# One 512-column matmul over the upper and lower part of the activations for each upper weight

## The chip, the cores and the metric

The kernel runs on 1 core of one Trainium2 chip. The metric is device time of one execution, in microseconds (us). Before the change it is 1568.76 us, the median of 3 runs (1565.63 to 1576.21).

## The reference, cut to what matters

One decoder block over 256 tokens of width 2048 (batch 1, one layer). All large products are of float32 weights with float32 activations:

```
mod = silu(c) @ w_mod + b_mod                  # six vectors of 2048
h   = rms_norm(x) * (1 + sc1) + sh1
q, k, v, u, gate_a, gate_s = split(h @ w_in)   # 1024 each for q, k, v, u; 2048 for each gate
y_attn = block-sparse attention of q, k, v     # 8 heads of 128
y_ssm  = y * sigmoid(y @ w_glu + b_glu)        # y from a diagonal state-space scan over u
x  = x + g1 * ((sigmoid(gate_a) * (y_attn @ w_attn_br) + sigmoid(gate_s) * (y_ssm @ w_ssm_br)) @ w_out)
h2 = rms_norm(x) * (1 + sc2) + sh2
val, gt = split(causal_conv3(h2 @ w_up))       # 5632 channels each
x  = x + g2 * ((silu(gt) * val) @ w_down)
```

## The kernel before

Activations lie transposed, channels on the 128 partitions and the 256 tokens along the row. To keep float32 accuracy, a product is made of three fp32r matmuls: weights and activations are both split into an upper part (rounded to fp32r) and a lower part (the rest), and upper by upper, upper weight by lower activation and lower weight by upper activation are added up in PSUM.

`chan_block` does this for 512 output channels. It goes over the contraction in steps of 256 rows, each step one weight tile of 128x1024 (512 KB). For each of four groups of 128 output channels (`m`) and two slices of 128 contraction rows (`k`) it issues

```
PE.matmul(p[m], hi[:, k, ms], act_hi(kk), ...)   # L264
PE.matmul(p[m], hi[:, k, ms], act_lo(kk), ...)   # L266
PE.matmul(p[m], lo[:, k, ms], act_hi(kk), ...)   # L268
```

so 24 matmuls of 256 columns in a step, each behind a weight load of its own. `tok_block` (q, k, v) has the activations as weights and the split weight as moving operand, in matmuls of 512 columns (L294 to L299).

The order of work is written out. `plan` holds all weight tiles; `go` takes them in turn. A tile is loaded on SP's queue into one of 5 `raw` buffers (`mraw`, 4 buffers, for the tiles of `w_mod` once the second pool is open), ScalarE makes `whi` (L182, `split_hi`), VectorE makes `wlo` (L187, `split_lo`), three steps ahead of the step that uses them (`WB` = 3). The tiles of `w_mod` are put between the steps at rates (`R_GLU` 0.6, `R_PPP` 0.4, `R_OUT` 0.9, `R_FFN` 0.34 tiles a step). From the GLU on, a tile of `w_mod` is a VectorE multiplication with `cb`, the broadcast silu(c) (L441); `cb` comes by a DMA on POOL's queue (L453). What belongs behind a block (`post`: sigmoid, convolution, gating, splitting the result again) is issued one step after the block's last step. Two PSUM buffers `mm` of 4 KB per partition hold the running block and the one before it. The compiler's scheduler may put instructions of one engine in another order than they are written, by its own time model, and then fixes it.

In order of time: modulation, u, k, q, v and gate_s (until 413 us), gate_a (`gap`), the attention branch (`pap`), the GLU (`glup`), the state-space branch (`ppp`), `w_out` (`outp`), the second norm, then the FFN (`gp` gate, `vp` value, `dp` down) in two halves, from 812 us to the end.

The pool `ssm` (scan) is closed before the GLU and the pool `post` is opened in its space; `cb`, `mraw` and the FFN tiles are in `post`. The 16 `head` tiles (attention) lie in the pool `act`, which stays open.

Of the kernel before, what the change touches and what calls it, by code (L numbers as in the profile page):

```python
# [23 lines left out]
HID = 5632  # L24
# [18 lines left out]
def block_kernel(ctx: ExitStack, tc: tile.TileContext, I, out):  # L43
# [6 lines left out]
    sm = ctx.enter_context(tc.tile_pool(name="sm", bufs=2))  # L50
    ps = ctx.enter_context(tc.tile_pool(name="ps", bufs=1, space=PSUM))
# [16 lines left out]
    def pair(kind, c, name, dt=F32R):  # L68

        return act.tile([128, 2, 256], dt, name=name, tag=f"{kind}{c}", bufs=1)  # L70

    def pairs(kind, c0, n, name):
        tiles = [pair(kind, c, name) for c in range(c0, c0 + n)]
        return lambda k: tiles[k // 2][:, k % 2]

    def head(name, dt=F32):
        return act.tile([128, 256], dt, name=name, tag="head", bufs=16)
# [201 lines left out]

    def tok_block(name, w, c0, kbs, act_hi, act_lo, post, k0=0, seed=None):  # L280
# [30 lines left out]
    HI, LO = [None] * 8, [None] * 8  # L311
    h_hi = lambda k: HI[k // 2][:, k % 2]
    h_lo = lambda k: LO[k // 2][:, k % 2]
# [14 lines left out]
    xT = [pair("lo", c, "xT", F32) for c in range(8)]  # L328
# [181 lines left out]
    def modulate(c, src, a, sh):  # L510

        t = w4("t", (128, 2, 256))
        for i in range(2):
            k = 2 * c + i
            V.scalar_tensor_tensor(t[:, i], src[:, i], a[:, k:k + 1], rb, op0=ALU.mult, op1=ALU.mult)
        HI[c], LO[c] = pair("hi", c, "hi"), pair("lo", c, "lo")
        for i in range(2):
            k = 2 * c + i
            A.activation(HI[c][:, i], t[:, i], AF.Identity, bias=sh[:, k:k + 1])  # L519
            V.scalar_tensor_tensor(LO[c][:, i], t[:, i], sh[:, k:k + 1], HI[c][:, i].bitcast(F32),  # L520
                                   op0=ALU.add, op1=ALU.subtract)
# [568 lines left out]
    def ga_post(b, p):  # L1090
        if b % 2 == 0:
            mA[b // 2] = e8("mA")
        A.activation(mA[b // 2][:, 4 * (b % 2):4 * (b % 2) + 4], p, AF.Sigmoid)
# [5 lines left out]
    split = {}  # L1099

    def two_parts(names, k, src):
        A.copy(split[names[0]](k), src)
        V.tensor_sub(split[names[1]](k), src, split[names[0]](k).bitcast(F32))
# [7 lines left out]
    for b in range(4):  # L1111
        with_mods(lambda: chan_block("gap", w_in, 4096 + 512 * b, 8, h_hi, h_lo, lambda p, b=b: ga_post(b, p)),
                  R_GAP if b else 0.0)
        go()
# [8 lines left out]
    split["yh"], split["yl"] = pairs("hi", 0, 4, "yh"), pairs("hi", 4, 4, "yl")  # L1123
    for ct in range(8):
        two_parts(("yh", "yl"), ct, uT[:, ct])
    ssm_ctx.close()
    post = ctx.enter_context(tc.tile_pool(name="post", bufs=1))
# [3 lines left out]
    split["sh"], split["sl"] = pairs("lo", 0, 4, "ysh"), pairs("lo", 4, 4, "ysl")  # L1131
    cb = silu_rows(post)

    def glu_post(b, p):
        sg4 = w4("sg", (128, 4, 256))
        for m in range(4):
            ct = 4 * b + m
            sg = sg4[:, m]
            A.activation(sg, p[:, m], AF.Sigmoid, bias=b_glu[:, ct:ct + 1])
            V.tensor_mul(sg, sg, uT[:, ct])  # L1140
            two_parts(("sh", "sl"), ct, sg)
# [6 lines left out]
    merged = {}  # L1148

    def pp_post(b, p):  # L1150
        if b == 0:
            merged["h0"], merged["l0"] = pairs("hi", 0, 4, "mh"), pairs("hi", 4, 4, "ml")
        if b == 2:
            merged["h1"], merged["l1"] = e8("mh", F32R), e8("ml", F32R)
        ms = slice(4 * (b % 2), 4 * (b % 2) + 4)
        t = w4("mt", (128, 4, 256))
        V.tensor_mul(t, p, sig_s[b // 2][:, ms])
        V.tensor_add(t, t, mA[b // 2][:, ms])
        for m in range(4) if b < 2 else ():
            split.update(mh=merged["h0"], ml=merged["l0"])  # L1160
            two_parts(("mh", "ml"), 4 * b + m, t[:, m])
        if b >= 2:
            A.copy(merged["h1"][:, ms], t)
            V.tensor_sub(merged["l1"][:, ms], t, merged["h1"][:, ms].bitcast(F32))

    m_hi = lambda k: merged["h0"](k) if k < 8 else merged["h1"][:, k - 8]
    m_lo = lambda k: merged["l0"](k) if k < 8 else merged["l1"][:, k - 8]
# [10 lines left out]
    for b in range(2):  # L1178
        with_mods(lambda: chan_block("glup", w_glu, 512 * b, 4, split["yh"], split["yl"],
                                     lambda p, b=b: glu_post(b, p)), R_GLU)  # L1180
    for b in range(4):
        with_mods(lambda: chan_block("ppp", w_s, 512 * b, 4, split["sh"], split["sl"],
                                     lambda p, b=b: pp_post(b, p)), R_PPP)
# [8 lines left out]
    def out_post(b, p, ms=(0, 1, 2, 3)):  # L1192
        for m in ms:
            k = 4 * b + m
            V.scalar_tensor_tensor(x2[k // 8][:, k % 8], p[m] if len(ms) < 4 else p[:, m], g1[:, k:k + 1],
                                   x2[k // 8][:, k % 8], op0=ALU.mult, op1=ALU.add)
        k = 4 * b + ms[0]
        squares(st2, range(k, k + len(ms)), x2[k // 8][:, k % 8:k % 8 + len(ms)], 2 if len(ms) == 4 else 0)

    for b in range(4):  # L1200
        with_mods(lambda: chan_block("outp", I["w_out"], 512 * b, 8, m_hi, m_lo,
                                     lambda p, ms=(0, 1, 2, 3), b=b: out_post(b, p, ms),
                                     groups=((0, 1), (2, 3)) if b == 3 else None), R_OUT)
        go()
# [13 lines left out]
    def conv(p, dst, m, ct):  # L1218
        A.activation(dst, p[:, m], AF.Identity, bias=conv_b[:, ct:ct + 1], scale=conv_w[:, 2, ct:ct + 1])
        V.scalar_tensor_tensor(dst[:, 1:256], p[:, m, 0:255], conv_w[:, 1, ct:ct + 1], dst[:, 1:256],  # L1220
                               op0=ALU.mult, op1=ALU.add)
        V.scalar_tensor_tensor(dst[:, 2:256], p[:, m, 0:254], conv_w[:, 0, ct:ct + 1], dst[:, 2:256],
                               op0=ALU.mult, op1=ALU.add)
# [3 lines left out]
    def gate_post(j, p):  # L1227
        gates[j] = post.tile([128, 4, 256], F32, name="gate", tag="gate", bufs=2)
        for m in range(4):
            conv(p, gates[j][:, m], m, 44 + 4 * j + m)  # L1230
            A.activation(gates[j][:, m], gates[j][:, m], AF.Silu)

    def val_post(j, n, p):
        val = post.tile([128, 4, 256], F32, name="val", tag="val", bufs=1)
        if n in (3, 4):
            rows = [[head("gh", F32R), head("gl", F32R)] for m in range(4)]
            gx[j] = lambda i, m: rows[m][i]
        else:
            g = e8("g", F32R, (128, 2, 4, 256)) if n < 3 else post.tile([128, 2, 4, 256], F32R, name="g", tag="g")
            gx[j] = lambda i, m: g[:, i, m]  # L1240
        for m in range(4):
            conv(p, val[:, m], m, 4 * j + m)
            V.tensor_mul(val[:, m], val[:, m], gates[j][:, m])
            A.copy(gx[j](0, m), val[:, m])
            V.tensor_sub(gx[j](1, m), val[:, m], gx[j](0, m).bitcast(F32))
# [3 lines left out]
    def down_post(hf, b, p, ms=(0, 1, 2, 3)):  # L1249
        for m in ms:  # L1250
            k = 4 * b + m
            xk = x2[k // 8][:, k % 8]
            V.scalar_tensor_tensor(xk, p[m] if len(ms) < 4 else p[:, m], g2[:, k:k + 1], xk,
                                   op0=ALU.mult, op1=ALU.add)
        if hf == 1:
            k, n = 4 * b + ms[0], len(ms)
            DMA.dma_start(osrc[:, k:k + n], x2[k // 8][:, k % 8:k % 8 + n])

    def up_pair(j, n):
        with_mods(lambda: chan_block("gp", w_up, HID + 512 * j, 8, h_hi, h_lo, lambda p: gate_post(j, p)), R_FFN)  # L1260
        with_mods(lambda: chan_block("vp", w_up, 512 * j, 8, h_hi, h_lo, lambda p: val_post(j, n, p)), R_FFN)
# [24 lines left out]


# [64 lines left out]
```

## Time and profile before

| | |
|---|---|
| median of 3 runs | 1568.76 us |
| the profiled execution | 1572.68 us, its span 1570.9 us |
| TensorE matmul / weight load busy | 1519.6 us (97%) / 1391.9 us (89%) |
| VectorE, ScalarE busy | 1013.0 us (64%), 802.6 us (51%) |
| read from HBM | 350.83 MB, 225 GB/s over the span |
| mean granted TensorE clock | 0.991 of full speed |

A busy TensorE tells only that some matmul is under way, not at what pace: the pace is read from the starts of single matmuls. Shares over the whole span mix stages with different limits, so the stages are looked at one by one.

### The profile page before, as it was taken

The page shows a single profiled execution, that of the slowest core. Times are in us where ns is not written, and L with a number is a line of the kernel's source. Part 1 is how long each engine was busy: PE and PEld are TensorE (multiplying, and loading weights), DVE is VectorE, ACT ScalarE, POOL GpSimd, SP SyncE. Part 2 cuts the span into 40 slices and gives each one's busy share as a digit, 9 for nine tenths or more (in the row PEclk, how much of TensorE's full clock was granted, in tenths as well). Part 3 has the DMA queues.
Part 4 walks back from the last instruction along what each step waited for, and adds up shares of the span by engine and source line. Part 5 has one row for each costly group of instructions (what it writes and reads, how often), then busy time and mean ns, then how long its engine had stood idle before and what let it go on. Part 6 is the DMA issues. An engine that isn't in the chain of part 4 may idle for free.

```text
span 1570.9 us, 30129 instructions
## 1 busy us (share of the span) xinstructions
PE 1519.6 (97%) x12376; PEld 1391.9 (89%) x12376; DVE 1013.0 (64%) x1740; ACT 802.6 (51%) x1162; POOL 11.3 (1%) x25
## 2 busy tenths in 40 slices
PE   7999999999998999999989999999999999999999
PEld 4666768689986879999969999999999999999999
DVE  2786344877664457988677787776444566655644
ACT  3676657976754434643345455455333444554432
POOL 1000000000000000000000000000000000000000
PEclk9999999999999999999999999999999999999999
DMA  8887777634356767879777666675555555555563
GB/s 319 281 307 279 249 272 267 247 127 134 127 184 237 246 244 257 300 280 336 260 263 252 249 244 246 245 244 180 185 188 178 185 187 178 186 185 180 200 195 114
DMA packets 99226, 354.90 MB, mean 226 GB/s; under 512 B 10928, under 2 KB 13104, under 8 KB 98960
## 3 DMA queue, kind: packets, MB, share of 16 engines
q1 hardware_dynamic: 97760, 348.17, 63.8%
q0 software_dynamic: 1184, 4.66, 0.8%
q8 instruction: 97, 1.59, 0.4%
q14 instruction: 41, 0.34, 0.1%
q10 hardware_dynamic: 144, 0.14, 0.0%
HBM read 350.83 MB, written 2.10 MB: 225 GB/s over the span
## 4 chain that ended last, share of the span: by engine, by line
PE 70%; DVE 8%; DMA 7%; ACT 4%; issue 1%; SPq 0%; ACTq 0%; DVEq 0%; POOLq 0%
PE vp L268 5%; PE vp L266 5%; PE vp L264 5%; PE dp L268 5%; PE dp L264 5%; PE dp L266 5%; PE gp L266 5%; PE gp L264 5%; PE gp L268 5%; DMA raw<-in_w_in_dram 4%; DVE wlo L187 3%; PE outp L264 2%; PE outp L266 2%; PE outp L268 2%; ACT whi L182 2%
## 5 line engine op out<-in xcount | busy, mean ns | idle before, releaser
L187 DVE TENSOR_TENSOR wlo<-raw,whi 128x1024 fp32r<-128x1024 f32 x464 | 567.1, 1224 | 452.8 <-ACT whi L182 452.0
L182 ACT CAST whi<-raw 128x1024 fp32r<-128x1024 f32 x464 | 485.4, 1048 | 629.1 <-PE dp L266 142.3
L264 PE MATMUL gp<-hi,whi 128*128 128x256 f32 x704 | 199.4, 283 | 0.0
L264 PE MATMUL vp<-hi,whi 128*128 128x256 f32 x704 | 199.2, 283 | 0.0
L266 PE MATMUL vp<-lo,whi 128*128 128x256 f32 x704 | 199.2, 283 | 0.0
L268 PE MATMUL vp<-hi,wlo 128*128 128x256 f32 x704 | 199.2, 283 | 0.0
L266 PE MATMUL gp<-lo,whi 128*128 128x256 f32 x704 | 199.2, 283 | 0.0
L268 PE MATMUL gp<-hi,wlo 128*128 128x256 f32 x704 | 199.2, 283 | 0.0
L264 PEld LDWEIGHTS gp<-hi,whi 128*128 128x128 f32 x704 | 135.1, 192 | 1.0 <-ACT hi L519 1.0
L264 PEld LDWEIGHTS vp<-hi,whi 128*128 128x128 f32 x704 | 135.2, 192 | 0.0
L266 PEld LDWEIGHTS vp<-lo,whi 128*128 128x128 f32 x704 | 135.2, 192 | 0.0
L268 PEld LDWEIGHTS vp<-hi,wlo 128*128 128x128 f32 x704 | 135.2, 192 | 0.0
L266 PEld LDWEIGHTS gp<-lo,whi 128*128 128x128 f32 x704 | 135.1, 192 | 0.0
L268 PEld LDWEIGHTS gp<-hi,wlo 128*128 128x128 f32 x704 | 135.1, 192 | 0.0
L268 PE MATMUL dp<-g,wlo 128*128 128x256 f32 x448 | 126.7, 283 | 0.0
L264 PE MATMUL dp<-g,whi 128*128 128x256 f32 x448 | 126.6, 283 | 0.0
L266 PE MATMUL dp<-g,whi 128*128 128x256 f32 x448 | 126.5, 282 | 0.0
L441 DVE SCALAR_TENSOR_TENSOR mraw<-mraw,cb 128x1024 f32<-128x1024 f32 x64 | 78.1, 1221 | 15.3 <-DMA mraw<-in_w_g_dram 10.6
L266 PEld LDWEIGHTS dp<-g,whi 128*128 128x128 f32 x448 | 85.8, 191 | 0.0
L264 PEld LDWEIGHTS dp<-g,whi 128*128 128x128 f32 x448 | 85.8, 191 | 0.0
L268 PEld LDWEIGHTS dp<-g,wlo 128*128 128x128 f32 x448 | 85.7, 191 | 0.0
L264 PE MATMUL gap<-hi,whi 128*128 128x256 f32 x256 | 76.2, 298 | 3.1 <-ACT whi L182 3.1
(341 smaller groups left out, 3464.2 us busy)
## 6 DMA issues: line engine op xcount, KB each, us to landing
raw<-in_w_up_dram SPq DMA_DIRECT2D x176, 512.0 KB, 3.7
raw<-in_w_in_dram SPq DMA_DIRECT2D x128, 512.0 KB, 4.5
raw<-in_w_m_dram SPq DMA_DIRECT2D x120, 512.0 KB, 4.9
raw<-in_w_down_dram SPq DMA_DIRECT2D x88, 512.0 KB, 3.3
mraw<-in_w_g_dram SPq DMA_DIRECT2D x64, 512.0 KB, 4.9
raw<-in_w_out_dram SPq DMA_DIRECT2D x32, 512.0 KB, 5.1
raw<-in_w_attn_br_dram SPq DMA_DIRECT2D x16, 512.0 KB, 4.1
raw<-in_w_ssm_br_dram SPq DMA_DIRECT2D x16, 512.0 KB, 5.2
```

The source lines that it names most:

```text
L182: A.copy(hi, loaded[i][0])
L187: V.tensor_sub(lo, loaded[i][0], hi_lo[i][0].bitcast(F32))
L264: follow(PE.matmul(p[m], hi[:, k, ms], act_hi(kk), start=first and m in starts, stop=False, skip_group_check=True))
L266: PE.matmul(p[m], hi[:, k, ms], act_lo(kk), start=False, stop=False, skip_group_check=True)
L268: PE.matmul(p[m], lo[:, k, ms], act_hi(kk), start=False, stop=u == kbs - 1 and k == 1, skip_group_check=True)
L441: V.scalar_tensor_tensor(flat, flat, 1.0, cb[:, 1024 * half:1024 * half + 1024], op0=ALU.mult, op1=ALU.mult, accum_out=sums[:, k, half:hal ...
```

## The change

The upper and the lower part of an activation slice lie side by side (`[.., 2, 256]`, upper first). The new `joint_block` does 256 output channels in steps of 512 contraction rows (the weight tile is again 128x1024, 512 KB, laid out anew on the host). For each of two groups `m` and four slices `k` it issues one matmul of 512 columns, upper weight by both parts, and one of 256 columns, lower weight by the upper part. The PSUM tile holds both sums; `both_sums` copies the second half out with ScalarE and adds the first with VectorE. A block of 256 channels has half the steps that one of 512 had, so that the number of steps and of weight tiles stays as it was, and `post` comes twice as often for half the channels.

It is used for `gap`, `glup`, `ppp`, `outp`, `gp`, `vp` and `dp`; `chan_block` stays for u, gate_s, `pap` and the first gate block of the FFN. In the last block of `outp` and of the last `dp`, each `m` has a PSUM tile of its own and its two sums are added to x by two operations in turn (`add_to`). The posts work on two channel groups at once (128x512) where they had worked on one or four. In `ppp` the second and third step change places. The `head` tiles get a pool of their own, which is closed before `post` is opened, and `post` takes that space too. xT and the normed activations now share tiles.

The diff, cut to its core:

```diff
+    head_ctx = ExitStack()
+    hp = head_ctx.enter_context(tc.tile_pool(name="heads", bufs=1))
...
+    def pair(c, name, dt=F32R):
+        return act.tile([128, 2, 2, 256], dt, name=name, tag=f"hl{c}", bufs=1)
...
     def head(name, dt=F32):
-        return act.tile([128, 256], dt, name=name, tag="head", bufs=16)
+        return hp.tile([128, 256], dt, name=name, tag="head", bufs=16)
...
+    def joint_block(name, w, b, kbs, act, post, k0=0, groups=None):
+        st = {}
+        def step(u, hi, lo):
+            if u == 0:
+                if groups:
+                    st["m"] = [make([128, 2, 256], name) for make in (mm_tile, bu_tile)]
+                else:
+                    st["p"] = mm_tile([128, 2, 2, 256], name)
+                    st["m"] = [st["p"][:, m] for m in range(2)]
+            p = st["m"]
+            hi4, lo4 = (a.rearrange("p a (b n) -> p (a b) n", n=256) for a in (hi, lo))
+            for m in range(2):
+                ms = slice(128 * m, 128 * m + 128)
+                for k in range(4):
+                    a = act(k0 + 4 * u + k)
+                    follow(PE.matmul(joined(p[m]), hi4[:, k, ms], joined(a), start=u == 0 and k == 0,
+                                     stop=False, skip_group_check=True))
+                    PE.matmul(p[m][:, 0], lo4[:, k, ms], a[:, 0], start=False, stop=u == kbs - 1 and k == 3,
+                              skip_group_check=True)
+                if groups and u == kbs - 1:
+                    post(p[m][:, None], (m,))
+            if u == kbs - 1 and not groups:
+                later(1, lambda: post(st["p"], (0, 1)))
+        for u in range(kbs):
+            add_weights(w[k0 // 4 + u, b], lambda hi, lo, u=u: step(u, hi, lo))
+
+    def both_sums(p, make=None):
+        n = p.shape[1]
+        t = make(n) if make else post.tile([128, 2, 256], F32, name="ts", tag="ts", bufs=2)[:, 0:n]
+        A.copy(t, p[:, :, 1])
+        V.tensor_add(t, t, p[:, :, 0])
+        return t
+
+    def add_to(x, k0, p, g):
+        n = p.shape[1]
+        for s in (p[:, :, 0], p[:, :, 1]) if n == 1 else (both_sums(p),):
+            for m in range(n):
+                k = k0 + m
+                xk = x[k // 8][:, k % 8]
+                V.scalar_tensor_tensor(xk, s[:, m], g[:, k:k + 1], xk, op0=ALU.mult, op1=ALU.add)
...
     ssm_ctx.close()
+    head_ctx.close()
     post = ctx.enter_context(tc.tile_pool(name="post", bufs=1))
...
     def glu_post(b, p):
+        sg = both_sums(p)
+        for m in range(2):
+            A.activation(sg[:, m], sg[:, m], AF.Sigmoid, bias=b_glu[:, 2 * b + m:2 * b + m + 1])
+        V.tensor_mul(sg, sg, uT[:, 2 * b:2 * b + 2])
+        two_parts(gt[b], sg)
...
     def pp_post(b, p):
+        ms = slice(2 * (b % 4), 2 * (b % 4) + 2)
+        t = both_sums(p)
+        V.tensor_mul(t, t, sig_s[b // 4][:, ms])
+        V.tensor_add(t, t, mA[b // 4][:, ms])
+        two_parts(merged[b], t)
...
+    def gate_post(j, i, p):
+        if i == 0:
+            gates[j] = post.tile([128, 4, 256], F32, name="gate", tag="gate", bufs=2)
+        gate = gates[j][:, 2 * i:2 * i + 2]
+        conv(both_sums(p), gate, 44 + 4 * j + 2 * i)
+        A.activation(gate, gate, AF.Silu)
+
+    def val_post(j, n, i, p):
...
+        val = post.tile([128, 2, 256], F32, name="val", tag="val", bufs=2)
+        conv(both_sums(p), val, 4 * j + 2 * i)
+        V.tensor_mul(val, val, gates[j][:, 2 * i:2 * i + 2])
+        two_parts(gx[j][:, 2 * i:2 * i + 2], val)
```

## Rows read from the trace of the kernel before

**Rows 1.** the page's first part (busy time of each engine) and a line of its second part (granted clock in 40 slices).

```profile
PE 1519.6 (97%) x12376; PEld 1391.9 (89%) x12376; DVE 1013.0 (64%) x1740; ACT 802.6 (51%) x1162; POOL 11.3 (1%) x25
...
PEclk9999999999999999999999999999999999999999
```

**Rows 2.** busy time of each engine in stretches: `gap`, the 47 steps from `glup` to two thirds of `outp`, the rest of `outp`, the FFN with tiles of `w_mod` between its steps and without. Columns: from and to, length, then busy us and instructions of PE, PEld, DVE, ACT, POOL, granted clock, DMA share, GB/s.

```profile
412.60:558.30 145.70, 137.33 (x1290) 116.69 (x1288) 83.01 (x146) 71.17 (x110) 0.00 (x0) 0.96 0.62 214
624.00:763.00 139.00, 136.37 (x1134) 134.51 (x1133) 118.90 (x194) 65.52 (x78) 2.85 (x4) 1.00 0.87 314
763.00:791.20 28.20, 28.20 (x239) 27.66 (x237) 14.46 (x20) 10.39 (x10) 0.00 (x0) 1.00 0.62 202
812.00:1083.00 271.00, 271.00 (x2260) 271.00 (x2260) 209.26 (x338) 137.65 (x190) 0.00 (x0) 1.00 0.69 239
1083.00:1567.00 484.00, 484.00 (x4039) 484.00 (x4038) 271.89 (x333) 208.46 (x254) 0.00 (x0) 1.00 0.55 180
```

**Rows 3.** instructions in order of time, in the FFN: start us, duration us, engine, line, operation. The two matmuls are 24 matmuls apart.

```profile
900.01 0.28 PE L268 MATMUL gp<-hi,wlo 128*128 128x256 f32 x1
900.01 0.19 PEld L264 LDWEIGHTS gp<-hi,whi 128*128 128x128 f32 x1
902.89 0.28 PE L268 MATMUL gp<-hi,wlo 128*128 128x256 f32 x1
```

**Rows 4.** the same view in a `tok_block`, matmuls of 512 columns, each with a weight load of its own. These two are 15 matmuls apart.

```profile
284.88 0.39 PE L294 MATMUL qp<-whi,hi 128*128 128x512 f32 x1
288.28 0.39 PE L294 MATMUL qp<-whi,hi 128*128 128x512 f32 x1
```

**Rows 5.** groups of instructions of one shape: how many L264 matmuls (one for each `m` and `k`) each block name has. Columns: count, busy us, mean ns of one, idle time of the engine before them.

```profile
L264 PE MATMUL gap<-hi,whi 128*128 128x256 f32 x256 | 76.2, 298 | 3.1 <-ACT whi L182 3.1
L264 PE MATMUL glup<-yh,whi 128*128 128x256 f32 x64 | 18.2, 284 | 0.8 <-ACT whi L182 0.8
L264 PE MATMUL ppp<-ysh,whi 128*128 128x256 f32 x128 | 36.2, 283 | 0.0
L264 PE MATMUL outp<-mh,whi 128*128 128x256 f32 x256 | 72.7, 284 | 0.0
L264 PE MATMUL gp<-hi,whi 128*128 128x256 f32 x704 | 199.4, 283 | 0.0
L264 PE MATMUL vp<-hi,whi 128*128 128x256 f32 x704 | 199.2, 283 | 0.0
L264 PE MATMUL dp<-g,whi 128*128 128x256 f32 x448 | 126.6, 283 | 0.0
L264 PE MATMUL dp<-gh,whi 128*128 128x256 f32 x256 | 72.4, 283 | 0.0
```

**Rows 6.** operations on 512 elements a partition, from two tile views (durations ns, least/median/greatest): a VectorE operation with one operand in PSUM, and a ScalarE copy from PSUM.

```profile
L800 DVE TENSOR_TENSOR r<-bu,z_rot x16: 672/683/692, 277.4 to 598.9; 128x512 f32<-128x512 f32 x16
...
L411 ACT COPY rows<-modp x18: 372/586/590, 18.9 to 807.6; 128x512 f32<-128x512 f32 x14, 128x256 f32<-128x256 f32 x4
```

**Rows 7.** VectorE's groups from 620 to 790 us, columns as in rows 5.

```profile
L187 DVE TENSOR_TENSOR wlo<-raw,whi 128x1024 fp32r<-128x1024 f32 x57 | 69.5, 1222 | 19.7 <-ACT whi L182 19.6
L1157 DVE TENSOR_TENSOR mt<-ppp,sig_s 128x1024 f32<-128x1024 f32 x4 | 4.9, 1222 | 0.5 <-PE ppp L268 0.5
L1140 DVE TENSOR_TENSOR sg<-sg,u 128x256 f32<-128x256 f32 x8 | 3.0, 420 | 0.0
L1103 DVE TENSOR_TENSOR ysl<-sg,ysh 128x256 fp32r<-128x256 f32 x8 | 2.9, 422 | 0.0
L1164 DVE TENSOR_TENSOR ml<-mt,mh 128x1024 fp32r<-128x1024 f32 x2 | 2.4, 1217 | 0.0
```

**Rows 8.** the start of `cb`, from the timelines of POOL, ACT and PE. In brackets: idle time before it, and what ended it.

```profile
619.00 0.54 POOL L453 DMA_DIRECT2D cb<-in_c_dram  x1 [476.74 <-PE py L778]
...
627.89 1.92 ACT L454 ACTIVATE cb<-cb 128x2048 f32<-128x2048 f32 x1
...
624.00 0.28 PE L268 MATMUL pap<-yhi,wlo 128*128 128x256 f32 x1
...
630.79 0.39 PE L264 MATMUL glup<-yh,whi 128*128 128x256 f32 x1 [0.76 <-ACT whi L182]
```

**Rows 9.** busy time in stretches of 10 us, columns as in rows 2.

```profile
640.00:650.00 10.00, 9.10 (x76) 8.89 (x75) 9.64 (x19) 6.19 (x12) 0.00 (x0) 1.00 0.90 348
650.00:660.00 10.00, 10.00 (x83) 9.85 (x83) 9.94 (x23) 6.32 (x12) 1.43 (x2) 1.00 0.90 325
810.00:820.00 10.00, 10.00 (x86) 10.00 (x85) 10.00 (x21) 5.93 (x9) 0.00 (x0) 1.00 0.67 235
```

**Rows 10.** ScalarE in order of time beside a value post of the FFN.

```profile
900.80 0.56 ACT L1219 ACTIVATE val<-vp,p 128x256 f32<-128x256 f32 x1
902.73 1.05 ACT L182 CAST whi<-raw 128x1024 fp32r<-128x1024 f32 x1 [1.37 <-PE gp L266]
903.68 0.40 ACT L1244 CAST g<-val 128x256 fp32r<-128x256 f32 x1
```

**Rows 11.** the splits of `gap` on ScalarE and what ended their idle time, columns as in rows 5.

```profile
L182 ACT CAST whi<-raw 128x1024 fp32r<-128x1024 f32 x31 | 32.4, 1046 | 47.5 <-DMA raw<-in_w_in_dram 39.4 <-DMA raw<-in_w_attn_br_dram 2.7 <-PE gap L266 2.2
```

**Rows 12.** the end of the trace.

```profile
1567.38 0.28 PE L268 MATMUL dp<-gh,wlo 128*128 128x256 f32 x1
1567.70 0.48 DVE L1253 SCALAR_TENSOR_TENSOR x<-dp,g,x 128x256 f32<-128x256 f32 x1 [0.17 <-PE dp L268]
```

More of the change, by code (lines that the diff above doesn't have):

```diff
@@ L66, in e8, with pairs @@
         return act.tile(list(shape), dt, name=name, tag="e8", bufs=5)
[L68 to L73, printed above, removed]
+    def pair(c, name, dt=F32R):
+        return act.tile([128, 2, 2, 256], dt, name=name, tag=f"hl{c}", bufs=1)
+    def pairs(c0, n, name):
+        tiles = [pair(c, name) for c in range(c0, c0 + n)]
         return lambda k: tiles[k // 2][:, k % 2]
+    joined = lambda a: a.rearrange("p a n -> p (a n)")
     def head(name, dt=F32):
-        return act.tile([128, 256], dt, name=name, tag="head", bufs=16)
+        return hp.tile([128, 256], dt, name=name, tag="head", bufs=16)
     def w4(name, shape, dt=F32):
@@ L327, in block_kernel @@
     A.dma_start(p0, I["p0"])
-    xT = [pair("lo", c, "xT", F32) for c in range(8)]
+    xT = [pair(c, "xT", F32)[:, 0] for c in range(8)]
     for c in range(8):
@@ L1110, in block_kernel @@
     go()
[L1111 to L1114, printed above, removed]
+    for b in range(8):
+        with_mods(lambda: joint_block("gap", I["w_ga"], b, 4, h_of, lambda p, ms, b=b: ga_post(b, p)),
+                  R_GAP if b > 1 else 0.0)
+        if b % 2:
+            go()
     drain(gens["attn"])
@@ L1147, in block_kernel @@
         parts, rest = parts[4:], rest[1:]
-    merged = {}
+    merged = []
     def pp_post(b, p):
[L1151 to L1167, printed above, removed]
+        if b < 4:
+            merged.append(pair(b, "m"))
+        elif b % 2 == 0:
+            m4 = e8("m", F32R, (128, 4, 2, 256))
+            merged.extend((m4[:, 0:2], m4[:, 2:4]))
+        ms = slice(2 * (b % 4), 2 * (b % 4) + 2)
[3 more added lines that the diff above has]
+        two_parts(merged[b], t)
     x2 = []
@@ L1190, in block_kernel, with out_post @@
     st2 = {}
[L1192 to L1204, printed above, removed]
+    def out_post(b, p, ms):
+        k, n = 2 * b + ms[0], len(ms)
+        add_to(x2, k, p, g1)
+        squares(st2, range(k, k + n), x2[k // 8][:, k % 8:k % 8 + n], 2 if n == 2 else 0)
+    for b in range(8):
+        with_mods(lambda: joint_block("outp", I["w_out"], b, 4, of(merged),
+                                      lambda p, ms, b=b: out_post(b, p, ms), groups=b == 7), R_OUT)
+        if b % 2:
+            go()
     all_mods()
@@ L1216, in block_kernel @@
         mods += gate_block(5, 4 * j, 4, cb, g2)
[L1218 to L1223, printed above, removed]
@@ L1225, in block_kernel @@
-    gates, gx = {}, {}
[L1227 to L1245, printed above, removed]
```

110 lines of the change are left out of this document (65 added, 45 removed).

## The prediction

> **What bounds the kernel now.** I read four views in this order: the page's busy times with the granted clock, the busy times by stretch, the starts of single matmuls, and the groups of VectorE's work.
>
> The page says that TensorE bounds the kernel and that its clock is no issue: matmuls busy 97% of the span, granted clock at full speed in nearly every slice [rows 1]. In the FFN, from 812 us on, TensorE is busy in all of 271 + 484 us [rows 2], so what a matmul costs there is what the kernel costs. In the 139 us from `glup` into `outp` VectorE is busy for 118.9 us (86%), beside TensorE's 136.4 [rows 2]; there two engines are near their limit. In `gap` TensorE is busy for 137.3 of 145.7 us [rows 2], and ScalarE's splits idled for 39.4 us until a weight tile landed [rows 11]: loads limit part of that stage.
>
> The busy share hides the pace. In the FFN 24 matmuls of 256 columns take 902.89 - 900.01 = 2.88 us, 120.0 ns from start to start, each with a weight load [rows 3]. In `tok_block` 15 matmuls of 512 columns, also with a load each, take 3.40 us, 226.7 ns [rows 4]. Twice 120.0 is 240.0, so twice the columns cost 13.3 ns less in one instruction than in two. Between the two rows a column costs (226.7 - 120.0) / 256 = 0.417 ns, a column a cycle at 2.4 GHz; 256 columns are 106.7 ns, and 13.3 ns are left per instruction in both rows.
>
> **What the change takes away.** For each `m` and `k` three matmuls of 256 columns (360.0 ns) become one of 512 and one of 256. No row shows the two in turn. The bounds: the columns alone with one fixed cost, 768 x 0.417 + 13.3 = 333 ns; and no gain, 360 ns, if the load of the next weights can't be hidden behind the short one. I take the sum of the two rows, 226.7 + 120.0 = 346.7 ns, since both have a load for each matmul; 13.3 ns saved. The Trainium skill (TensorE: Matmul & The Clock Gate, section Back-to-back issue gap) has a smaller fixed cost, N/2.4 + 2.5 ns for a warm matmul; by that the saving would be 2.5 ns. The trace does not agree: 120.0 against 109.2 ns, 226.7 against 215.8.
>
> How often: the L264 counts are 256 (`gap`), 64 (`glup`), 128 (`ppp`), 256 (`outp`), 704 (`gp`), 704 (`vp`) and 448 + 256 (`dp`) [rows 5]. The first gate block (4 groups x 16 slices = 64) keeps its form. That leaves 2048 in the FFN and 704 before it, 2752 x 13.3 ns = 36.7 us if all of it reached the end.
>
> **FFN: -27.3 us** (2048 x 13.3 ns). What must stay hidden is the new work: for each half block a ScalarE copy of 128x512 from PSUM, 0.59 us, and a VectorE addition with a PSUM operand, 0.68 us [rows 6]. A half block lasts 4 steps, 4 x 8 x 346.7 ns = 11.1 us. VectorE's share is now 209.3 / 271 = 77% in the part with `w_mod` tiles [rows 2]; 0.68 per 11.1 us adds 6 points, the shorter step 3, and 512-element operations in place of two of 256 (0.68 against 2 x 0.42 [rows 6, 7]) give a little back: about 85%. At 810 us VectorE is busy for 10.0 of 10 us and TensorE loses nothing [rows 9], so I cost it at nothing; without that cover it would be the first rival. The PSUM tile of a half block is wanted again one half block (11.1 us) later, and copy and addition are done some 3 us after its end, behind one `whi` and one `wlo`. ScalarE has 138 of 271 us busy [rows 2].
>
> **`gap`: -1.7 us.** 256 x 13.3 ns = 3.4 us is the most; nothing, if the landing loads set the pace [rows 11]. I take half. The extra table loads that eight sigmoids may bring in place of four lie on ScalarE, which is busy for 71 of 145.7 us [rows 2].
>
> **`glup` to two thirds of `outp`: +1.5 us.** 368 of the pairs (46 steps of 8) would give 4.9 us here. But VectorE gets more work. In `glup` two channel groups cost it 4 x 0.42 = 1.68 us before (a product and a subtraction each) and 3 x 0.68 after: +0.37, four times, 1.5 us. In `ppp` a 512-channel post costs 2 x 1.22 + 4 x 0.42 = 4.1 us in two blocks and 3 x 1.22 = 3.7 in two, 15.6 in all [rows 7]; after, 8 x 4 x 0.68 = 21.8: +6.2. In `outp` six additions, +4.1. Together 118.9 + 11.8 = 130.7 us of VectorE, in a stretch that TensorE alone would need 136.4 - 4.9 = 131.5 us for. Two engines at the same load that wait for each other don't both get through without idling: they needed 139 us with 119 and 136. So I expect none of the 4.9 us. On top, `cb`: its DMA waited 477 us until the last matmul of the scan, whose pool had been where `post` now lies [rows 8]. With the head tiles' space also under `post`, it waits for the last reader of those, the last `pap` matmul at 624.0 instead of 619.0 [rows 8], 5 us later, and all VectorE's `w_mod` work waits for `cb`. Already now the first splits queue behind it on ScalarE, and TensorE stands for 0.76 us [rows 8]. Bounds of the late `cb`: 0, if spare buffers take it up, and +5 us. I take 1.5.
>
> **The rest of `outp`: -1.1 us.** 10 steps, 80 pairs; TensorE is busy all through and VectorE half [rows 2].
>
> **The end: +0.5 us.** The last matmul is followed by one VectorE operation of 0.48 us [rows 12]; now two in turn, one for each sum. At the end of `outp` it is the same, but a square over half as much follows, so I leave that at 0. xT and the normed activations share tiles, so the first upper part waits for both products of a slice, not for one; the lower part waited for both before. 0, at most 1 us.
>
> **Unchanged:** loads (same tiles, same bytes, same number of steps), u, k, q, v, gate_s, `pap`. DMA share in the FFN is 0.55 to 0.69 [rows 2], so a step that is 4% shorter is fed.
>
> **Sum:** -27.3 - 1.7 + 1.5 - 1.1 + 0.5 = -28.1 us. Against the profiled execution (1572.68 us, its span 1570.9) that is 1544.6. This execution stands 3.9 us over the median of the runs, 1568.76; against the median it is 1540.7, and I predict 1541 us.
>
> **Rivals.**
> - *Late lower weights in the FFN (slower).* The post is now a longer chain: copy, addition, two activations, four VectorE operations, product, cast, subtraction, between ScalarE and VectorE in turn. Where the scheduler puts a `whi` behind its last link, that `wlo` is late. From the rows: `whi` 1.05 [rows 10], copy 0.59, addition 0.68, activations and convolution some 2, product 0.68, cast 0.6, subtraction 0.68, then `whi` 1.05 and `wlo` 1.22: 8.5 us, against 3 steps of 2.77 = 8.3 us of lead. One `w_mod` tile in between, 1.22 us, makes it late by a microsecond. There are about 130 posts; 0.22 us lost at each eats the gain, from 0.34 us on the kernel is over 1% slower, at 0.5 us it is 1541 + 65 = 1606 us. For it: VectorE at 96% and TensorE at 9.1 in 640 to 650 [rows 9]. Against it: in the trace the scheduler puts a `whi` between the links of a value post [rows 10], and TensorE stays full beside a full VectorE [rows 9]. 7%.
> - *The pair saves nothing.* If the load behind a short matmul sets 120 ns and the long one pays for two loads, the pair is 360 ns and only the additions remain: 1568.76 + 1.5 + 4.9 + 0.5, about 1575 us. For it: weight loads cover TensorE's whole time in the FFN [rows 2]. Against it: the long matmul with its own load is at 226.7 [rows 4]. 6%. By the Trainium skill's 2.5 ns (same page and section) the saving would be 2752 x 2.5 ns = 6.9 us, an estimate of 1562 us.
> - *All of it arrives.* VectorE keeps up in `glup` to `outp`, `gap` follows TensorE: 1568.76 - 36.7 + 0.5 = 1532.6 us. For it: in the last 28 us of `outp` VectorE is only half busy [rows 2], so work that slips into them costs nothing. Against it: that asks for a lag of some ten microseconds, and four `mraw` buffers allow four operations. 17%.
> - *VectorE bounds `glup` to `outp`.* It needs 130.7 us from when `cb` arrives, 5 us later, and idles as much as now (139 - 118.9 = 20 us): 5 + 131 + 20 = 156 us instead of 139, less what of the idling falls away, half perhaps; +8 to +17 us in place of +1.5, so 1548 to 1556 us. For it: 9.94 of 10 us at 650 [rows 9]. Against it: TensorE was full there. 12%.
>
> **How the numbers follow.** Forecast 58% (1535 to 1548), and the rivals as given. A change of this kernel can be told from none from about 1% on, 15.7 us: 1553 to 1584 are the same. Faster: 58 + 17 + 9 of the last rival's 12, less 2 for small losses at the posts, 82%. Same: 6 + 3 + 2 = 11%. Slower 7%. The range takes in the full gain and most of the fourth rival: 1530 to 1553.
>
> **What would show it right or wrong.** In the FFN, starts 226.7 and 120.0 ns apart in turn, and steps of 2.77 us; TensorE without idle time between 830 us and the end. From `glup` into `outp` VectorE busy for about 131 us and the stretch as long as before; `cb`'s DMA behind the last `pap` matmul. In the FFN no wait of TensorE for `wlo`. A pair at 360 or 333 ns, or a wait at every post, would make the prediction wrong.

## The result, and the profile after

After the change the kernel takes 1550.58 us (median of 4 runs, 1546.88 to 1553.8), before it 1569.32 us in the same series: a ratio of 0.9875, 95% interval 0.9834 to 0.9916. The profiled execution is at 1551.37 us with a span of 1549.6, against 1572.68 and 1570.9. So it is 18.7 us (1.2%) faster by the medians and 21.3 by the profiles; 28.1 were forecast. The interval lies below 1, so the gain is clear of the spread. 1550.58 lies inside the stated range (1530 to 1553), but above the band of the forecast itself (1535 to 1548).

The page's first part after the change, and the granted clock:

```profile
PE 1491.3 (96%) x9624; PEld 1239.2 (80%) x9624; DVE 1052.7 (68%) x1778; ACT 847.4 (55%) x1201; POOL 11.3 (1%) x25
...
PEclk9999999999999999999999999999999999999999
```

There are 2752 matmuls and as many weight loads fewer than in [rows 1], exactly the number of pairs. TensorE's share hardly fell.

To see where the time went, the two traces are cut at the first matmul of each stage (us):

| | first matmul of `gap` | `gap` | `pap` | `glup` | `ppp` | `outp` to `gp` | `gp` to the end |
|---|---|---|---|---|---|---|---|
| before | 412.6 | 145.7 | 65.8 | 26.5 | 46.2 | 108.8 | 765.3 |
| after | 416.5 | 137.6 | 66.0 | 28.5 | 46.7 | 109.4 | 744.9 |
| difference | +3.9 | -8.1 | +0.2 | +2.0 | +0.5 | +0.6 | -20.4 |

The first column holds stages that the change did not touch. Over the 14 profiled executions of this study it lies between 409.0 and 420.3 us, so a difference of 4 us there is spread. In what follows a version is measured from the first `gap` matmul to the end of its span as well: 1158.3 us before, 1133.1 after, 25.2 less. All stage times are those of one profiled execution a version.

Busy times after the change in stretches, columns as in [rows 2]: `gap`; `glup`; `ppp`; the next 66 us of `outp`; its rest; the FFN with tiles of `w_mod` and without:

```profile
416.50:554.10 137.60, 132.41 (x1034) 98.93 (x1032) 88.71 (x155) 78.71 (x121) 0.00 (x0) 1.00 0.64 226
620.00:648.50 28.50, 23.91 (x130) 20.61 (x130) 19.76 (x32) 17.60 (x22) 0.54 (x1) 0.94 0.83 297
648.50:695.20 46.70, 45.09 (x258) 39.12 (x257) 46.49 (x71) 26.24 (x35) 1.43 (x2) 1.00 0.75 261
695.20:761.00 65.80, 65.58 (x371) 54.41 (x369) 59.44 (x106) 28.44 (x33) 1.42 (x2) 1.00 0.90 336
761.00:791.40 30.40, 30.27 (x171) 24.70 (x171) 19.41 (x29) 14.08 (x16) 0.00 (x0) 1.00 0.72 254
811.00:1074.20 263.20, 262.70 (x1537) 230.17 (x1536) 217.91 (x345) 147.83 (x190) 0.00 (x0) 1.00 0.72 243
1074.00:1546.00 472.00, 471.45 (x2718) 415.57 (x2716) 289.91 (x347) 226.95 (x268) 0.00 (x0) 1.00 0.58 187
```

In the FFN TensorE stays full and VectorE is at 218 of 263 us (83%; 85% was forecast). In `glup` TensorE is busy for only 23.9 of 28.5 us. In `ppp` VectorE has no idle time left (46.49 of 46.70 us).

The pace of the pair in the FFN, which answers to [rows 3], near 960 us and near 1300 us:

```profile
960.64 0.40 PE L302 MATMUL gp<-hl,whi 128*128 128x512 f32 x1
960.87 0.28 PE L304 MATMUL gp<-hl,wlo 128*128 128x256 f32 x1
960.99 0.40 PE L302 MATMUL gp<-hl,whi 128*128 128x512 f32 x1
...
961.70 0.40 PE L302 MATMUL gp<-hl,whi 128*128 128x512 f32 x1
...
1300.10 0.39 PE L302 MATMUL vp<-hl,whi 128*128 128x512 f32 x1
1300.33 0.28 PE L304 MATMUL vp<-hl,wlo 128*128 128x256 f32 x1
1300.45 0.39 PE L302 MATMUL vp<-hl,whi 128*128 128x512 f32 x1
...
1301.14 0.39 PE L302 MATMUL gp<-hl,whi 128*128 128x512 f32 x1
```

At 1300 us three pairs take 1.04 us, 346.7 ns each, the sum of the two rows of before. At 960 us three pairs take 1.06 us, 353.3 ns. Both paces last: the slow one from 829.5 to 1087.5 us (some 730 pairs), the fast one from 1087.8 us to the end.

The waits of TensorE from 600 to 705 us: who waited, for what, us in total, times, longest:

```profile
PE glup L302 <- DVE ts L319: 4.6, 1, 4.6
PE ppp L302 <- DVE yg L1155: 0.8, 1, 0.8
PE ppp L302 <- DVE ts L319: 0.8, 1, 0.8
PE outp L302 <- DVE m L1155: 0.2, 1, 0.2
```

The longest of them in order of time, with what it hangs on (ScalarE, VectorE, TensorE and POOL by start; answers to [rows 8]):

```profile
620.86 0.54 POOL L505 DMA_DIRECT2D cb<-in_c_dram  x1 [477.22 <-PE pap L272]
...
628.64 1.28 ACT L506 ACT_TABLE_LOAD   x1 [4.63 <-DMA cb<-in_c_dram]
629.93 1.91 ACT L506 ACTIVATE cb<-cb 128x2048 f32<-128x2048 f32 x1
631.75 1.03 ACT L186 CAST whi<-raw 128x1024 fp32r<-128x1024 f32 x1
632.68 0.58 ACT L318 COPY ts<-glup 128x512 f32<-128x512 f32 x1
...
631.88 1.23 DVE L493 SCALAR_TENSOR_TENSOR mraw<-mraw,cb 128x1024 f32<-128x1024 f32 x1 [6.61 <-ACT cb L506]
...
635.37 0.68 DVE L319 TENSOR_TENSOR ts<-ts,glup 128x512 f32<-128x512 f32 x1
...
636.11 0.80 PE L302 MATMUL glup<-y,whi 128*128 128x512 f32 x1 [4.59 <-DVE ts L319]
```

`cb`'s DMA now starts behind the last `pap` matmul and lands 7.7 us later. ScalarE waits 4.63 us for it, and behind its silu stand the next `whi` and the copy of the first GLU block. Until the addition behind that copy has run, the third GLU block has no PSUM tile. Inside the GLU this wait could not arise before: the GLU had two blocks for two PSUM buffers, now it has four. Around its end the granted clock falls, to 0.94 on the mean of `glup`.

The end, which answers to [rows 12]:

```profile
1545.18 0.28 PE L304 MATMUL dp<-g,wlo 128*128 128x256 f32 x1
1545.49 1.00 DVE L329 SCALAR_TENSOR_TENSOR x<-dp,g,x 128x256 f32<-128x256 f32 x2 [0.38 <-PE dp L304]
```

From the start of the last matmul to the end of the span 4.4 us pass; before it was 3.5.

### The profile page after: what moved, and what is told of

The parts are those of the page before. It is cut to its first block, busy times and chain, and to the rows that moved or that the text cites. A ratio compares the mean times of both kernels' runs of the same rounds, so it can differ in the third digit from the quotient of the medians.

```text
span 1549.6 us, 24718 instructions
## 1 busy us (share of the span) xinstructions
PE 1491.3 (96%) x9624; PEld 1239.2 (80%) x9624; DVE 1052.7 (68%) x1778; ACT 847.4 (55%) x1201; POOL 11.3 (1%) x25
## 4 chain that ended last, share of the span: by engine, by line
PE 78%; DVE 8%; DMA 8%; ACT 5%; issue 2%; SPq 0%; ACTq 0%; DVEq 0%; POOLq 0%
PE vp L302 10%; PE dp L302 10%; PE gp L302 10%; PE dp L304 5%; PE vp L304 5%; PE gp L304 5%; DMA raw<-in_w_in_dram 3%; PE outp L302 3%; DVE wlo L191 3%; PE modp L456 3%; PE gap L302 3%; ACT whi L186 2%; PE ppp L302 2%; PE outp L304 2%; PE gap L304 2%
## 5 line engine op out<-in xcount | busy, mean ns | idle before, releaser
L302 PE MATMUL vp<-hl,whi 128*128 128x512 f32 x704 | 247.2, 395 | 0.5 <-DVE gate L1272 0.5
L302 PE MATMUL dp<-g,whi 128*128 128x512 f32 x704 | 244.5, 391 | 0.0
L302 PE MATMUL gp<-hl,whi 128*128 128x512 f32 x640 | 224.5, 395 | 0.0
L304 PE MATMUL vp<-hl,wlo 128*128 128x256 f32 x704 | 197.4, 280 | 0.0
L304 PE MATMUL gp<-hl,wlo 128*128 128x256 f32 x640 | 179.5, 280 | 0.0
L302 PEld LDWEIGHTS vp<-hl,whi 128*128 128x128 f32 x704 | 132.0, 188 | 31.8 <-issue 0.8
L302 PEld LDWEIGHTS gp<-hl,whi 128*128 128x128 f32 x640 | 120.0, 187 | 28.1
L304 PEld LDWEIGHTS vp<-hl,wlo 128*128 128x128 f32 x704 | 133.0, 189 | 0.0
L304 PEld LDWEIGHTS gp<-hl,wlo 128*128 128x128 f32 x640 | 120.9, 189 | 0.0
L302 PE MATMUL gap<-hl,whi 128*128 128x512 f32 x256 | 93.9, 406 | 0.6 <-ACT whi L186 0.5
```

The lines of the kernel that those rows point to most:

```text
L302: follow(PE.matmul(joined(p[m]), hi4[:, k, ms], joined(a), start=u == 0 and k == 0, stop=False, skip_group_check=True))
L304: PE.matmul(p[m][:, 0], lo4[:, k, ms], a[:, 0], start=False, stop=u == kbs - 1 and k == 3, skip_group_check=True)
```

## The experiments

All ratios stand against the kernel before, measured beside each run on the same chip. "Run 3" in the text is the third experiment; "gap to end" is the profiled time from the first `gap` matmul to the end of the span (before 1158.3, after 1133.1).

**1. The changed kernel again, unchanged.**

> The changed kernel once more, unaltered. In its first profile a pair of matmuls (512 and 256 columns) takes 353.3 ns from 829 to 1087 us and 346.7 ns from there to the end. If the program sets this pace, the same stretches show the same two paces and the run is within 0.3% of 1551 us. If it falls by chance, the stretches are divided otherwise, and the time moves by up to 2048 x 6.7 ns = 14 us between executions.

1550.79 us (one execution), gap to end 1132.9. Two parts moved against each other: `glup` takes 31.8 us instead of 28.5, and the FFN 740.4 instead of 744.9. In its FFN the fast pace begins at 846.0 us and holds to the end. The same instructions thus run at either pace. The 700 pairs behind 841.5 us in the first execution x 6.67 ns are 4.7 us, about the difference of the two FFNs (4.5).

**2. The 512-column matmul as two of 256, all else as after.**

```diff
-PE.matmul(joined(p[m]), hi4[:, k, ms], joined(a), ...)
+PE.matmul(p[m][:, 0], hi4[:, k, ms], a[:, 0], ...)
+PE.matmul(p[m][:, 1], hi4[:, k, ms], a[:, 1], ...)
```

> The changed kernel with the 512-column matmul issued as two of 256 columns (upper part into the first sum, lower part into the second); layout, posts, additions and pools stay. If the width of the matmul is the gain, three starts are 120 ns apart again (360 ns), 2048 triples in the FFN cost 2048 x (360 - 350) = 20 us more and the stages before some 4 to 7: about 1575 us, slower than the kernel before by the cost of the additions (0 to 10 us). If the gain came from the layout, the fused posts or the smaller blocks, the time stays at about 1551 us.

Three triples in the FFN of this run:

```profile
960.03 0.28 PE L302 MATMUL gp<-hl,whi 128*128 128x256 f32 x1
...
961.11 0.28 PE L302 MATMUL gp<-hl,whi 128*128 128x256 f32 x1
```

1576.86 us, ratio 1.0038 (1.0018 to 1.0058); gap to end 1163.7. A triple takes 360.0 ns again, and the FFN 765.5 us, as long as before (765.3), though all copies, additions and new posts are in it. So the new work costs next to nothing in the FFN, and the whole gain there comes from the width. From `glup` to `gp` it takes 189.4 us against 181.5: there the new posts do cost something. `gap` is at 141.9, so 3.8 of its 8.1 us were not the width's: in the execution before, TensorE stood for the split of a late weight tile and then ran for a time at the lower level of its clock (1.2 GHz), as these rows of before show (a wait, then columns as in [rows 2]; clock 0.73). After the change and in this run the clock in `gap` was 1.00.

```profile
480.16 0.39 PE L264 MATMUL gap<-hi,whi 128*128 128x256 f32 x1 [2.71 <-ACT whi L182]
...
476.00:486.00 10.00, 6.47 (x30) 3.57 (x23) 4.79 (x9) 6.28 (x8) 0.00 (x0) 0.73 0.69 242
```

**3. From `glup` to `outp` three matmuls of 256 columns into one sum, without copy and addition; the FFN and `gap` as after.**

```diff
+PE.matmul(p[m][:, 0], hi4[:, k, ms], a[:, 0], ...)
+PE.matmul(p[m][:, 0], hi4[:, k, ms], a[:, 1], ...)
-    sg = both_sums(p)
...
```

> In the GLU, the state-space branch and w_out the three products go into one sum by three 256-column matmuls, without copy and addition behind; the FFN and gate_a stay as changed. If the additions on VectorE ate the gain there, these 56 steps get shorter by some 3 to 5 us (171 us from the first GLU matmul to the last of w_out in the changed kernel, 167 in the one before) although TensorE works longer: about 1547 us. If TensorE's pace is the limit there too, they get longer by 448 x 10 ns = 4.5 us: about 1555 us.

1547.11 us, 0.9841 (0.9807 to 0.9875); gap to end 1136.4. `glup` to `gp` 186.5 us against 184.6 after and 187.7 in run 1: no gain of the wide matmul over its posts shows here. From the first GLU matmul to the last of `outp` it takes 174.5 us against 171.3 and 174.0, so these steps did not get shorter; the median came out at the 1547 us of the first reading without its cause. In this profile gap to end is 3.3 us longer than after. `ppp` has no stall any more (all steps 2.88 us). `glup` keeps its stall of 4.4 us, now behind the sigmoid that reads the PSUM tile: copy and addition were only the last links of that chain.

**4. `cb` in a pool of its own in the scan's space.**

```diff
+cbp = ctx.enter_context(tc.tile_pool(name="cbp", bufs=1, side="right"))
 head_ctx.close()
-    cb = silu_rows(post)
+    cb = silu_rows(cbp)
```

> The broadcast silu(c) gets a place of its own in the space of the scan, outside the head tiles' space, so that its DMA waits for the scan's last matmul and not for the last of the attention branch. If the late DMA is what stalls TensorE for 5 us in the GLU, the GLU is shorter by 3 to 5 us and the kernel at about 1547 us; if VectorE's later work takes that back, the GLU is shorter and the time to the end of w_out the same (1550 us); if another wait causes the stall, nothing changes.

```profile
616.92 0.53 POOL L505 DMA_DIRECT2D cb<-in_c_dram  x1 [473.56 <-PE py L830]
```

1550.99 us, 0.9861 (0.9839 to 0.9883). The DMA waits for the scan's last matmul again, as in [rows 8], and `glup` to `gp` falls to 182.4 us. `glup` itself is at 27.2 us, against 28.5 and 31.8: the wait for a PSUM tile is gone, but another has come, as before the change. ScalarE still stands for `cb`, three splits queue behind the silu, and TensorE waits for the first of them:

```profile
625.32 1.28 ACT L506 ACT_TABLE_LOAD   x1 [5.06 <-DMA cb<-in_c_dram]
626.61 1.91 ACT L506 ACTIVATE cb<-cb 128x2048 f32<-128x2048 f32 x1
628.43 2.92 ACT L186 CAST whi<-raw 128x1024 fp32r<-128x1024 f32 x3
...
629.51 0.50 PE L302 MATMUL glup<-y,whi 128*128 128x512 f32 x1 [1.76 <-ACT whi L186]
```

So the late DMA is one part of the stall, the place of the silu in ScalarE's order the other. gap to end is 1133.2, no better: `gap` took 2.6 us more than after, and the FFN had the slow pace again (744.9).

**5. The squares of two `outp` blocks given to TensorE together.**

```diff
-squares(st2, range(k, k + n), x2[...], 2 if n == 2 else 0)
+squares(st2, range(k, k + n), x2[...], 2 if n == 2 else 0, b in (0, 2, 4))
+if hold:
+    return
+held = st.pop("held")
```

> In w_out the squares of two neighbouring blocks go to TensorE together (four small float32 matmuls at once) after every second block, four interruptions of the fp32r stream in place of seven. If an interruption costs by itself (0.75 us each, with four small matmuls before the change and with two after it), three fewer make w_out 2.3 us shorter (109.4 us from its first matmul to the FFN's first). If the small matmuls themselves cost the time, their number is the same and w_out stays at 109 us.

1552.9 us, 0.9866 (0.9823 to 0.991). Not a gain: `outp` to `gp` took 110.6 us. Interruptions fell from 7 to 4, at 0.71 to 0.82 us each, but other steps of `outp` grew to 3.8 to 4.6 us. Inconclusive on its own; run 12 repeats it without such stalls.

**6. The silu of c four steps later, no tile of `w_mod` in the first two GLU blocks.**

```diff
-A.activation(cb, cb, AF.Silu)
+later(4, lambda: A.activation(cb, cb, AF.Silu))
...
-R_GLU)
+R_GLU if b > 1 else 0.0)
```

> No tile of w_mod in the first half of the GLU, and the silu of cb issued behind the fifth GLU step, so that the splits of these steps don't queue behind cb on ScalarE. If that queue is TensorE's stall of 5 to 7 us (steps of 7.6 and 4.2 us in place of 2.8), the GLU is at 23 to 25 us in place of 28.5 and 31.8, and the kernel at 1545 to 1547 us. If VectorE's load is the limit, the time comes back in the next two stages, because the same w_mod work is done later: 1550 us.

In this run and in run 8 one tile of `w_mod` is multiplied by c instead of silu(c). 1550.23 us, 0.9864 (0.9837 to 0.9892). `glup` 25.8 us, but `ppp` 50.7; what was won came back in the next stage.

**7. For two slices at a time both upper weights first, then both lower ones.**

```diff
-for k in range(4):
-    ... upper k; lower k
+for k2 in (0, 2):
+    ... upper k2, upper k2 + 1; lower k2, lower k2 + 1
```

> Of two slices, first both 512-column matmuls, then both of 256 columns. If each instruction has its own fixed cost of 13.3 ns, two pairs take 2 x 346.7 = 693.3 ns in any order, and the time is that of the changed kernel (1551 us) less what the slower rhythm of 353.3 ns a pair costs (up to 4.6 us in the first half of the FFN) if that rhythm comes from the alternation of the two lengths. If the load behind a short matmul is not hidden when another short one follows, it is slower.

1548.46 us, 0.985 (0.9823 to 0.9877); gap to end 1130.5. Most steps of the FFN are at 2.79 us, 348.7 ns a pair, and the FFN takes 742.2 us: one pace between the two. A fixed cost for each instruction, which would give 346.7 in any order, is thus not the whole account.

**8. Runs 4, 5 and 6 together.**

> The own place of cb, the paired squares and the later start of the w_mod tiles in the GLU together. If all three act and don't stand in for each other, the way from the first GLU matmul to the FFN's first is at 175 to 178 us (184.6 and 187.7 in the two profiles of the changed kernel, 181.5 before) and the kernel at about 1543 us. If VectorE limits this stretch, it stays over 182 us.

1547.1 us, 0.984 (0.9805 to 0.9875). `glup` 23.3 us, seven of its steps near 2.83 and one at 3.53: with an earlier `cb` and the silu out of the way the stall is gone. But `ppp` takes 51.9 us, and `glup` to `gp` 187.0, not the 175 to 178 of three edits that add up. TensorE's waits from 600 to 705 us, and VectorE in order of time:

```profile
PE ppp L302 <- DVE ts L319: 3.3, 1, 3.3
PE ppp L302 <- DVE yg L1160: 0.9, 1, 0.9
```

```profile
655.49 1.23 DVE L493 SCALAR_TENSOR_TENSOR mraw<-mraw,cb 128x1024 f32<-128x1024 f32 x1 [3.63 <-DMA mraw<-in_w_g_dram]
```

VectorE stands 3.63 us for a tile of `w_mod`, and the additions queue behind that multiplication. POOL's loads of x were under way at the time (first at 648.1 us); that they held the tile up is not shown.

**9 to 11. Three edits put together.** Run 9 joins runs 3 and 7. Run 10 is run 6, with the `w_mod` tiles counted from zero so that none comes ahead of the silu, and with the loads of x spread out:

```diff
-X_AT = (12, 17, 26, 30)
+X_AT = (20, 28, 34, 40)
+place["mod"] = 0.0
```

Run 11 joins runs 9 and 10.

> In the GLU, the state-space branch and w_out the products go in 256-column matmuls into one sum, without copies and additions; and in all joint blocks two upper-weight matmuls come in a row, then the two lower ones. If the two edits add up: FFN (gp to the end) 742 us as with the order alone, glup to gp about 186 us, steps of the FFN all 2.79 us, total 1544 to 1547 us. If the rhythm of the FFN falls by chance even in this order, its steps are 2.77 or 2.83 us and the FFN is anywhere from 740 to 745.

> The silu of c is written four steps later and no w_mod tile is placed in the first two GLU blocks; the loads of x are spread from step 20 on instead of 12. Theory (the splits queue behind the silu on ScalarE; what came back in ppp came from the x loads in front of a w_mod tile): glup near 23.3 us without a long step, ppp 47 us without the 6 us step, glup to gp about 181 us, total 1544 to 1547. Rival (VectorE has too little time for the postponed w_mod tiles, whichever loads run): glup 23.3 us, but ppp 50 us or more, or outp longer by the same, total as after the change, 1549 to 1551.

> Both edits together: 256-column matmuls in the three stages, the order of two upper then two lower, the later silu and the later loads of x. If the theory of the loads holds and VectorE, freed of 16 additions, keeps up: glup 23.5, ppp 46, outp 111, glup to gp about 181 us, FFN 742 us, total 1539 to 1543 us. If VectorE is short of time whatever is moved: glup to gp 186 us and 1544 to 1547 us.

Run 9: 1543.29 us, 0.9821 (0.9794 to 0.9848), gap to end 1127.3, FFN 742.7, `glup` to `gp` 184.5: the two edits add up. Run 10: 1545.33 us, 0.9828 (0.9796 to 0.986), gap to end 1126.9, FFN 739.7 at the fast pace. Run 11: 1541.74 us, 0.9809 (0.9788 to 0.9831), gap to end 1128.1, FFN 742.8.

Run 10 keeps one stall of 3 us in `glup` (25.9 us in all; the scheduler left the silu ahead of the copy). `ppp` is at 46.7, not 50.7, without the wait for a tile of `w_mod`; but since the stall came back with it, the loads of x are not shown to have been the cause in runs 6 and 8. `outp` to `gp` grew to 112.3 us by three long steps (3.63, 3.91, 4.18), so `glup` to `gp` is 184.9 us, no shorter than after: for the sum the rival holds. The rival's total was 1549 to 1551 us; 1545.33 lies in the range of the other reading, but these stages did not bring it.

Run 11 has the total that was expected (1539 to 1543 us), but not for the reason given: the silu stands ahead of the GLU's post on ScalarE again, `glup` takes 28.1 us instead of 23.5, and `glup` to `gp` 184.8 instead of 181. By gap to end run 10's edits add nothing to run 9.

```profile
PE glup L305 <- ACT ts L1200: 3.4, 1, 3.4
```

`ppp` and `outp` of run 11 run without any wait of TensorE up to the norm, so that the interruptions by the square sums stand alone: seven steps of 3.52 us, six of them followed by one of 2.98 (behind the seventh comes the last step), all others 2.88. That is 0.64 + 0.10 = 0.74 us each.

**12. Run 11 with run 5's squares.**

> As the run with both edits (256-column matmuls in three stages, two upper then two lower, later silu, later loads of x), with the square sums of two blocks of w_out given to TensorE together: 4 interruptions instead of 7. There w_out ran without any other stall: 24 steps of 2.88 us, seven of 3.52 and the one behind each of 2.98, so 0.74 us an interruption. Theory (an interruption costs about 0.74 us whatever number of small matmuls it holds): w_out 3 x 0.74 = 2.2 us shorter, 108.3 us from its first matmul to the FFN's, total 1539 to 1540 us. Rival (the small matmuls cost by their number): each interruption 1.3 us, w_out 110.5 us as in that run, total 1541 to 1542.

1538.76 us, 0.9803 (0.9772 to 0.9833); gap to end 1127.3. `outp` to `gp` 108.6 us against 110.5 in run 11 (108.3 expected, 110.5 by the rival). One interruption of run 11 and one of this run, TensorE in order of time:

```profile
706.87 0.40 PE L313 MATMUL outp<-m,wlo 128*128 128x256 f32 x2
707.20 0.63 PE L542 MATMUL sqs<-sq,ones 128*32 128x256 f32 x4
707.76 0.38 PE L305 MATMUL outp<-m,whi 128*128 128x256 f32 x1
```

```profile
716.49 0.40 PE L313 MATMUL outp<-m,wlo 128*128 128x256 f32 x2
716.82 0.64 PE L547 MATMUL sqs<-sq,ones 128*32 128x256 f32 x8
717.38 0.38 PE L305 MATMUL outp<-m,whi 128*128 128x256 f32 x1
```

Four small matmul records or eight, the next `outp` matmul starts 0.56 us after their start. Between these two lengths the interruption is paid, not its length. The kernel before, with eight records in each, has the same steps (3.54 and 2.98 us).

This version has the lowest median of all, but its interval overlaps those of runs 9 to 11, and by gap to end runs 9 and 10 are as good (1127.3 and 1126.9). Its interval ends at 0.9833, where that of the changed kernel begins (0.9834). By gap to end it is 5.8 us ahead of the changed kernel; the rest of the 13.3 us between the two spans is the spread of the early stages (409.0 against 416.5 us).

## Why the prediction was right, and where its sizes failed

**The direction and its cause held.** A pair costs 346.7 ns in two thirds of the FFN, the sum of the two rows, not 333 and not 360. Run 2 takes only the width away, and the FFN falls back to 765.5 us. The rival of late lower weights did not come: no wait of TensorE for `wlo` shows in the FFN, and its new posts cost one wait of 0.5 us. That rival was priced by "about 130 posts"; the trace has 57 copies of FFN blocks, so a late post would have had to cost more than twice what the prediction says to eat the gain. The rival by which the pair saves nothing fell with it. The formula that the prediction takes from the Trainium skill (TensorE: Matmul & The Clock Gate, section Back-to-back issue gap) is given there for a single matmul by itself, and the page says that it does not fit a stream of weight loads and matmuls. The rows that the prediction holds against it are such a stream.

**The hit is in part luck.** Two misses of 6.4 us cancelled: the FFN with the end gave less than forecast, `gap` more, and 3.8 us of `gap` came from one execution. What is left is 2.7 us lost in `glup` to `gp` and 3.9 in stages that the change did not touch. And the range went up to 1553 us for a rival whose mechanism did not come.

**The FFN term (-27.3 us) was mis-sized.** From `gp` to the end it was -20.4 us with the end's loss of 0.9 in it, so the FFN gave -21.3. The step that failed is "I take the sum of the two rows" for all 2048 pairs: some 730 of them ran at 353.3 ns, 4.9 us. The other 1.1 us are not assigned in full; 0.5 of them is a wait behind the first gate block. Where the fast pace came early (runs 1, 6 and 10) the FFN took 739.7 to 740.4 us, with the late one (after, runs 3, 4, 5 and 8) 744.2 to 745.5.

**`gap` (-1.7 us): too small.** It was -8.1; 141.9 - 137.6 = 4.3 us of it goes with the width by run 2 (both at a clock of 1.00), and 3.8 is a stall of the one execution of before. 4.3 is more than the 3.4 that I called the most; TensorE also waited less for late splits, 1.4 us against 3.0 in run 2. The same `gap` took 137.2 to 140.2 us in the other runs, the longer times with a fall of the clock in it, so these shares are good to some 2 us. Half was held back for landing loads; little of it had to be.

**`glup` to `gp` (+1.5 - 1.1 = +0.4 us): the sum was near, the reason wrong.** It was +3.1, and +6.2 in run 1. The step that failed is "two engines at the same load that wait for each other don't both get through without idling": behind two stalls in its first four steps, `ppp` ran eleven steps in a row at 2.77 us with VectorE full. VectorE's work was sized rightly, but it did not have to fit: 19.8 + 46.5 + 59.4 = 125.7 us of it fell in this stretch where 130.7 were worked out, and 5 us slipped into the rest of `outp` (19.4 us busy against 14.5 before), where TensorE was busy for 30.3 of 30.4 us. Over both parts it is 11.7 us more, with 11.8 worked out. The width's gain did arrive step by step, and was lost at places:
- *`cb`.* The DMA came behind the last `pap` matmul, as forecast. But its price did not go through the `w_mod` tiles on VectorE, to which I had tied it. It went through ScalarE's order and the PSUM tile of the first GLU block. Eight steps of 2.77 us are 22.2, so `glup` lost 6.3 us, 4.6 by the wait and most of the rest by the lower clock behind it; before it lost 26.5 - 8 x 2.88 = 3.5.
- *Two stalls of 0.8 us in `ppp`* (steps of 3.78 and 3.75 us), for the longer chain of posts: in run 3, without copy and addition, all steps of `ppp` are at 2.88.
- *The square sums in `outp`.* Blocks half as wide bring them to TensorE seven times instead of three within the stream: 4 x 0.74 = 3.0 us, about all that the width gives there (256 x 13.3 ns = 3.4). This was left out of the forecast, under "the rest of `outp`: -1.1 us" too.

**The end: +0.5 us** was +0.9.

**The rival that VectorE bounds `glup` to `outp`** has a time (1548 to 1556 us) that holds the measured one, but its mechanism did not come: that stretch lost 3 us (6 in run 1), not 8 to 17, and it did not get shorter in run 3, where VectorE has the additions no more. The rival by which all of it arrives fell on these same places.

## What to carry to other kernels

One wide matmul in place of two saved 13.3 ns of 360 here, in the stages that TensorE alone bounds; take that price from starts in the trace, and allow for a second pace (6.7 ns more a pair here). When a block is halved, count again everything that comes once a block: the PSUM tiles wanted at once (4.6 us here), and each small matmul put into the stream, which here cost 0.74 us by the interruption, with four records or eight. A stage that loses to its posts what it wins in matmuls can keep the old form beside the new one: runs 3 and 9 lost nothing by it from `glup` to `gp` that stands out of the spread (186.5 and 184.5 us against 184.6 and 187.7).

## What was not expected of the hardware

The same pair of matmuls runs at 346.7 or 353.3 ns, and keeps its pace for hundreds of microseconds. What sets it is open. In each of these profiles TensorE waits once for 0.5 us behind the first gate block; here the changed kernel, then run 1:

```profile
841.50 0.47 PE L302 MATMUL vp<-hl,whi 128*128 128x512 f32 x1 [0.50 <-DVE gate L1272]
```

```profile
845.57 0.47 PE L302 MATMUL vp<-hl,whi 128*128 128x512 f32 x1 [0.51 <-DVE gate L1272]
```

All eight profiles with this order of matmuls begin the FFN's pairs at the slow pace. Behind this restart five run on slow and three fast (runs 1, 6 and 10). In all five the slow pace ends without any stall behind the same pair, the first of the fourth step of `dp` (1087.8 us here), the first step that reads a `g` tile from the pool `post`. In `outp` of the changed kernel steps of 2.77 and 2.83 us come by turns between most of the interruptions by the square sums. So both a restart and a fixed place in the program can change the pace; how was not tried. With two upper weights in a row there was one pace alone, 348.7 ns, in all four runs with that order (FFN 742.2 to 742.8 us).
